# A hybrid S5 / DeltaNet step in which tanh results stay in PSUM, per-head scalings run on ScalarE, inverse blocks are copied into zeroed tiles, and the S5 scan is laid out by place

## The chip, the core and the metric

The kernel runs on one NeuronCore of a Trainium2 chip. The metric is the device time of one execution in microseconds, as the median of several runs. Engines have the profile's names: PE is TensorE (PEld its weight loads), DVE is VectorE, ACT is ScalarE, POOL is GpSimd, SP issues the DMAs.

## The reference

One layer of a bidirectional hybrid backbone works on 2048 latent tokens and 128 context tokens, all in float32. Cut to what matters here:

```python
proj = jnp.dot(h, w_in)                          # u, z_s5, qkv, z_gdn, beta, a
# S5, per direction d: 32 groups of 64 complex states, over the tokens
h[t] = abar * h[t-1] + (b_re + i*b_im) @ u[t]    # complex, h[-1] = h0
y[t] += c_re @ h_re[t] - c_im @ h_im[t]
s5 = gelu(y + u * d_skip) * sigmoid(z_s5)
# gated DeltaNet, per direction: 4 heads of 128, over chunks
q, k, v = split(silu(conv3(qkv)))
m = tril_strict((k * beta) @ k.T * exp(gcum_i - gcum_j))
t_inv = inverse(eye + m)                         # then one state update a chunk
out = concat(s5, gdn) @ w_out; x += gate * out; x += gate * mlp(x)
```

The outputs are both token blocks after a last norm and the context's final states. In the reference the DeltaNet chunks have 64 tokens; the kernel's have 128.

## The kernel before

A first pass makes the normalized tokens, splits them into a high and a low float32r part, stores both in DRAM, and computes u; beside it `s5_setup` and `s5_tables` make the S5 tables and store them (`sp`, `stab`). A second stage computes the other projections in token groups: `group_proj` takes a column tile of the input weights (split the same way, stored in DRAM once and loaded again for later groups), runs 24 matmuls into a PSUM bank of the tile `d` (L471), and `evac` empties it. For q, k and v `evac` applies a three-tap convolution and SiLU: ACT scales the middle tap (L491), DVE adds the two others (L493, L495), ACT takes tanh (L497), DVE combines (L499), and the result goes to DRAM.

Beside the projections run, in steps interleaved by generators with rates (`Side`): the S5 scan (`s5_part`, eight parts of four groups), the first half of DeltaNet (`gdn_first`: transposes, key products, decays; `gdn_p2`: inversion of 32x32 diagonal blocks on DVE; `gdn_p3`: assembling the 128x128 inverses on PE) and later the chunk steps (`gdn_load`, `gdn_step`). The last stage is the output projection and the MLP, with the remaining chunk steps in its beginning. The framework orders each engine's queue by a simulated timeline; an engine then works its queue in order.

`s5_part` covers 2176 tokens as 272 columns of 8 tokens. WI @ u fills S (L1283, evacuated by L1287): eight rows of 272 (direction, re/im, group pair). The rows are cut into 17 blocks of 16 places. Step 1 runs over the places: for `kk` 1 to 15, all 17 blocks at once are multiplied (L1301) and added twice (L1303, L1305), so these instructions take every 16th element. Step 2 carries the state over the blocks, 15 serial steps of three small instructions on `Hin` (L1323 to L1326). Step 3 adds carry times power to every place: POOL multiplies (L1335), DVE adds (L1338), eight times. Then a few state columns are overwritten (L1343, L1344), and L1356 reads the rows out as the moving operand of CA, with L1351 for the direct part; ACT and DVE apply gelu.

In `gdn_back` ACT makes the decays E (L696), POOL multiplies them by beta (L697), DVE multiplies by the key products (L700). In `gdn_p3` POOL writes the diagonal 32x32 blocks RW into the block tiles TA and R by multiplying with block masks Mh and Mb (L762, L764), which also writes the zeros. In `gdn_load` POOL scales the keys of a loaded chunk (L873).

Of the kernel before, what the change touches and what calls it, by code (L numbers as in the profile page):

```python
# [478 lines left out]
def evac(k, ct, ps, n, segs, off):  # L479
# [71 lines left out]
def gdn_setup(k):  # L551

    nc = k.nc
    k.Mb = k.ga.tile([128, 4], F32, name="Mb")
# [14 lines left out]
    nc.gpsimd.memset(k.Mb, 0.0)  # L569
    nc.gpsimd.memset(k.Mh, 0.0)  # L570
    for b in range(4):
        nc.gpsimd.memset(k.Mb[32 * b:32 * b + 32, b:b + 1], 1.0)
        nc.gpsimd.memset(k.Mh[32 * b:32 * b + 32, b % 2:b % 2 + 1], 1.0)
# [108 lines left out]
def gdn_back(k, b, c):  # L682
# [6 lines left out]
    for d in range(2):  # L689
# [7 lines left out]
        nc.gpsimd.tensor_tensor(E, E, bc4(bb[:, d]), op=OP.mult)  # L697
# [51 lines left out]
def gdn_p3(k, cs):  # L749
# [114 lines left out]
def gdn_load(k, c, d, second):  # L864
# [180 lines left out]
def s5_setup(k):  # L1045
# [208 lines left out]
def s5_part(k, hb):  # L1254
# [617 lines left out]
```

## Time and profile before

| | |
|---|---|
| median of 3 runs | 3313.9 us (3308.9 to 3318.6) |
| the profiled execution | 3305.3 us |
| its span | 3303.5 us |
| mean granted clock of PE over the span | 0.95 |

The span is what the profiler recorded from the first instruction to the last; the profiled execution is one run, and its durations are those that the rows below show. An instruction's row gives its line in the kernel, the engine, what it writes and reads, and partitions x elements. "Idle before" is the time in which the engine stood still ahead of such instructions, with the releasers after it.

### The profile page before, as it was taken

The page shows a single profiled execution, that of the slowest core. Times are in us where ns is not written, and L with a number is a line of the kernel's source. Part 1 is how long each engine was busy: PE and PEld are TensorE (multiplying, and loading weights), DVE is VectorE, ACT ScalarE, POOL GpSimd, SP SyncE. Part 2 cuts the span into 40 slices and gives each one's busy share as a digit, 9 for nine tenths or more (in the row PEclk, how much of TensorE's full clock was granted, in tenths as well). Part 3 has the DMA queues.
Part 4 walks back from the last instruction along what each step waited for, and adds up shares of the span by engine and source line. Part 5 has one row for each costly group of instructions (what it writes and reads, how often), then busy time and mean ns, then how long its engine had stood idle before and what let it go on. Part 6 is the DMA issues. An engine that isn't in the chain of part 4 may idle for free.

```text
span 3303.5 us, 53799 instructions
## 1 busy us (share of the span) xinstructions
PE 2998.2 (91%) x19962; PEld 2637.7 (80%) x19962; DVE 2060.2 (62%) x4093; ACT 1115.0 (34%) x2517; POOL 1370.5 (41%) x1027
## 2 busy tenths in 40 slices
PE   5775879999798899988999999999999999999998
PEld 3673668787787777977997899898798898899997
DVE  4965587896876775346555368543368652685555
ACT  3432224443443221245323243322243332432332
POOL 3552232433345242155443453434444444554442
PEclk8887889998997999998999999999999999999999
DMA  9899966867677988999333545222435334453322
GB/s 258 197 179 250 335 205 228 266 217 236 201 217 233 285 286 273 345 307 312 107 103 112 156 147 178 81 76 92 143 99 184 112 102 127 155 166 93 99 90 71
DMA packets 573527, 604.69 MB, mean 183 GB/s; under 512 B 163020, under 2 KB 422208, under 8 KB 573264
## 3 DMA queue, kind: packets, MB, share of 16 engines
q1 hardware_dynamic: 573264, 601.25, 59.4%
q8 instruction: 157, 2.57, 0.3%
q14 instruction: 106, 0.87, 0.1%
HBM read 458.99 MB, written 142.14 MB: 182 GB/s over the span
## 4 chain that ended last, share of the span: by engine, by line
PE 56%; DVE 19%; DMA 14%; issue 4%; ACT 3%; POOL 3%; SPq 2%; POOLq 0%; DVEq 0%; ACTq 0%
PE gA L1523 20%; PE gA L1545 18%; PE d L471 6%; PE gA L1437 3%; PE gs L1356 1%; DVE W L738 1%; DVE Tt L1301 1%; DMA x<-in_posr 1%; DVE UB L736 1%; DMA woraw<-in_w_out 1%; DVE S L1338 1%; PE gs L1283 1%; POOL wol L1400 1%; DVE S L1303 1%; DMA s_stab<-WI 1%
## 5 line engine op out<-in xcount | busy, mean ns | idle before, releaser
L1400 POOL TENSOR_TENSOR wol<-woraw,woh 128x512 fp32r<-128x512 f32 x320 | 426.3, 1343 | 679.9 <-ACT woh L1399 669.5
L1530 DVE TENSOR_TENSOR r<-r 128x256 f32<-128x256 f32 (+1 forms) x256 | 290.7, 1168 | 363.8 <-ACT ffH L1529 363.6
L1399 ACT ACTIVATE woh<-woraw 128x512 fp32r<-128x512 f32 x320 | 194.4, 628 | 794.6 <-PE gA L1545 462.0
L1545 PE MATMUL gA<-woh,ffH 128*128 128x512 f32 x1088 | 426.8, 392 | 8.8 <-ACT r L1527 4.8
L1545 PE MATMUL gA<-woh,ffL 128*128 128x512 f32 x1088 | 425.3, 391 | 1.1 <-DVE ffL L1531 1.1
L1545 PE MATMUL gA<-wol,ffH 128*128 128x512 f32 x1088 | 424.2, 390 | 0.0
L1550 DVE TENSOR_TENSOR acc<-acc,gA 128x512 f32<-128x512 f32 x510 | 336.1, 681 | 123.7 <-PE gA L1545 123.6
L1400 POOL TENSOR_TENSOR wil<-wiraw,wih 128x1024 fp32r<-128x1024 f32 x128 | 318.9, 2491 | 148.5 <-PE gA L1523 111.6
L1523 PE MATMUL gA<-htH,wih 128*128 128x256 f32 (+1 forms) x2048 | 286.9, 292 | 6.0 <-DVE acc L1550 4.0
L1523 PE MATMUL gA<-htL,wih 128*128 128x256 f32 (+1 forms) x2048 | 284.8, 290 | 0.0
L1523 PEld LDWEIGHTS gA<-htH,wih 128*128 128x128 f32 x2048 | 273.0, 192 | 13.1 <-DVE acc L1550 6.3
L1523 PE MATMUL gA<-htH,wil 128*128 128x256 f32 (+1 forms) x2048 | 282.0, 290 | 0.0
L1523 PEld LDWEIGHTS gA<-htL,wih 128*128 128x128 f32 x2048 | 270.5, 192 | 0.9
L1523 PEld LDWEIGHTS gA<-htH,wil 128*128 128x128 f32 x2048 | 268.6, 191 | 0.1
L471 PE MATMUL d<-hH,wh 128*128 128x258 f32 (+3 forms) x1152 | 213.4, 327 | 51.5 <-DMA wh<-s_wc 15.9
L1545 PEld LDWEIGHTS gA<-woh,ffH 128*128 128x128 f32 x1088 | 204.8, 188 | 52.7 <-ACT r L1527 6.1
L471 PEld LDWEIGHTS d<-hH,wh 128*128 128x128 f32 x1152 | 180.2, 206 | 74.0 <-issue 31.4
L1545 PEld LDWEIGHTS gA<-wol,ffH 128*128 128x128 f32 x1088 | 204.7, 188 | 43.2
L1545 PEld LDWEIGHTS gA<-woh,ffL 128*128 128x128 f32 x1088 | 204.9, 188 | 41.4 <-DVE ffL L1531 1.9
L471 PE MATMUL d<-hL,wh 128*128 128x258 f32 (+3 forms) x1152 | 213.1, 320 | 2.7 <-DMA hL<-s_hL 2.7
L471 PE MATMUL d<-hH,wl 128*128 128x258 f32 (+3 forms) x1152 | 209.4, 319 | 4.6 <-DMA wl<-s_wc 4.6
L471 PEld LDWEIGHTS d<-hH,wl 128*128 128x128 f32 x1152 | 178.0, 201 | 18.2 <-issue 10.3
(387 smaller groups left out, 5340.0 us busy)
## 6 DMA issues: line engine op xcount, KB each, us to landing
wiraw<-in_w_mlp_in SPq DMA_DIRECT2D x128, 512.0 KB
woraw<-in_w_mlp_out SPq DMA_DIRECT2D x256, 256.0 KB
wl<-s_wc SPq DMA_DIRECT2D x68, 512.0 KB
wh<-s_wc SPq DMA_DIRECT2D x68, 512.0 KB
wada<-in_w_ada SPq DMA_DIRECT2D x48, 512.0 KB
KVr<-s_kv SPq DMA_DIRECT2D x34, 512.0 KB
Qr<-s_qkv SPq DMA_DIRECT2D x32, 512.0 KB
woraw<-in_w_out SPq DMA_DIRECT2D x64, 256.0 KB
```

Of the source, the lines that this page charges most:

```text
L471: nc.tensor.matmul(ps[:, 0:w], W_[:, kk, :], X_[kk][:, f:f + w], start=(n == 0), stop=(n == 23))
L736: nc.vector.tensor_tensor(tv, W[:, 0:i + 1, i:i + 1].to_broadcast([128, i + 1, m]), U2[:, i, None, i + 1:32].to_broadcast([128, i + 1, m]) ...
L738: nc.vector.tensor_tensor(wv, wv, tv, op=OP.subtract)
L1283: nc.tensor.matmul(ps[64 * par:64 * par + 64, 0:272], WI[:, d, ri, g, 64 * par:64 * par + 64], ub[:, 2 * g + par, :], start=True, stop=Tru ...
L1301: V.tensor_tensor(Tt.rearrange("p j (a s)->p j a s", a=8), sview(S, kk, [[0, 2], [272, 8], [16, 17]]), TB8[:, :, :, None].to_broadcast([12 ...
L1399: nc.scalar.activation(h[:, i:i + n], w, AF.Copy)
L1400: sub.tensor_tensor(l[:, i:i + n], w, h[:, i:i + n].bitcast(F32), op=OP.subtract)
L1437: nc.tensor.matmul(ps, X[:, q, s], W[:, kk, :], start=(q == 0 and m == 0), stop=(q == 7 and m == 2))
L1523: nc.tensor.matmul(ps[b][:, 0:w], W[:, kk, :], X[:, kk, b * w:b * w + w], start=(m == 0), stop=(m == 23))
L1530: nc.vector.tensor_tensor(r[:, 0:w], r[:, 0:w], r[:, 0:w], op=OP.mult)
L1545: nc.tensor.matmul(ps, X[:, s], W[:, hf], start=(m == 0), stop=(m == 3 * FB - 1))
L1550: nc.vector.tensor_tensor(accs[i][:, c], accs[i][:, c], ps, op=OP.add)
```

## The change

1. `evac`: tanh is written to the PSUM bank that the projection came from, and L499's successor reads it there; the SBUF tile is no longer used for it.
2. `gdn_back` and `gdn_load`: the multiplications by beta and by the key decay move from one POOL instruction over four heads to four ACT copies with a per-partition scale.
3. `gdn_p3`: TA and R become tiles that are zeroed once in `gdn_setup`; ACT copies the diagonal blocks to their places, 12 small copies for each pair of chunks. The masks go.
4. `s5_part`: a row is kept by place, 17 places of 17 columns (place 0 holds the state that enters a block, places 1 to 16 follow, the blocks being neighbours), rows are 289 long and ordered re/im, direction, group. The steps over places work on runs of 17 neighbours. The carry over blocks is a doubling scan of 4 steps with the 16th, 32nd, 64th and 128th block powers, on runs of 15, 14, 12 and 8. L1287's successor writes, and L1356's successor reads, the row in token order, that is, one element every 17.
5. `s5_setup`: five tables laid out for direct use instead of two; three complex products for the higher powers. The per-part table copies go.

```diff
@@ -493,10 +493,10 @@
-        th = k.pe.tile([128, k.pew], F32, name="ec2")
-        nc.scalar.activation(th[:, 0:n], y2[:, 0:n], AF.Tanh)
+        th = ps[:, 0:n]
+        nc.scalar.activation(th, y2[:, 0:n], AF.Tanh)
...
-        nc.vector.scalar_tensor_tensor(o_[:, 0:n], th[:, 0:n], 1.0, y2[:, 0:n], op0=OP.add, op1=OP.mult)
+        nc.vector.scalar_tensor_tensor(o_[:, 0:n], th, 1.0, y2[:, 0:n], op0=OP.add, op1=OP.mult)
@@ -551,8 +551,10 @@
+    k.TA = k.ga.tile([128, 2, 4, 64], F32, name="TA")
+    k.R = [k.ga.tile([128, 2, 4, 128], F32, name=f"R{d}") for d in range(2)]
+    for t in (k.TA, *k.R):
+        nc.gpsimd.memset(t, 0.0)
@@ -694,7 +691,8 @@
         for h in range(4):
...
-        nc.gpsimd.tensor_tensor(E, E, bc4(bb[:, d]), op=OP.mult)
+        for h in range(4):
+            nc.scalar.activation(E[:, h], E[:, h], AF.Copy, scale=bb[:, d, h:h + 1])
@@ -753,19 +751,19 @@
-    TA = k.ga.tile([128, 2, 4, 64], F32, name="TA")[:, 0:n]
-    R = [k.ga.tile([128, 2, 4, 128], F32, name=f"R{d}")[:, 0:n] for d in range(2)]
+    TA = k.TA[:, 0:n]
+    R = [r[:, 0:n] for r in k.R]
...
-        for d in range(2):
-            pairs, a, e = PAIRS[d]
-            nc.gpsimd.tensor_tensor(TA[a, j].rearrange("p h (b c)->p h b c", b=2), RW[a, j, d, 1, :, None, :].to_broadcast([64, 4, 2, 32]),
-                                    k.Mh[a, None, :, None].to_broadcast([64, 4, 2, 32]), op=OP.mult)
-            nc.gpsimd.tensor_tensor(R[d][:, j].rearrange("p h (b c)->p h b c", b=4), RW[:, j, d, 0, :, None, :].to_broadcast([128, 4, 4, 32]),
-                                    k.Mb[:, None, :, None].to_broadcast([128, 4, 4, 32]), op=OP.mult)
...
     def sl(blk):
...
+    for d in range(2):
+        pairs, a, e = PAIRS[d]
+        for blk in range(4):
+            nc.scalar.activation(R[d][sl(blk), :, :, sl(blk)], RW[sl(blk), :, d, 0], AF.Copy)
+            if sl(blk).start in (a.start, a.start + 32):
+                nc.scalar.activation(TA[sl(blk), :, :, sl(blk % 2)], RW[sl(blk), :, d, 1], AF.Copy)
...
     for d in range(2):
@@ -870,7 +868,8 @@
-    nc.gpsimd.tensor_tensor(KV[:, 0], KV[:, 0], bc4(k.kd[:, c, d]), op=OP.mult)
+    for h in range(4):
+        nc.scalar.activation(KV[:, 0, h], KV[:, 0, h], AF.Copy, scale=k.kd[:, c, d, h:h + 1])
@@ -1030,13 +1029,13 @@
-    k.tab8 = SP[:, 1088:1216].rearrange("p (j r c)->p j r c", j=2, r=2)
-    k.tabL = SP[:, 1216:1344].rearrange("p (j r c)->p j r c", j=2, r=2)
-    k.h0 = SP[:, 1344:1408].rearrange("p (r c)->p r c", r=2)
...
+    k.tabs = SP[:, 1088:1728].rearrange("p (e b j q)->p e b j q", e=5, b=8, j=2)
+    k.h0 = SP[:, 1728:1792].rearrange("p (r c)->p r c", r=2)
@@ -1124,11 +1123,20 @@
-    for t_, e in ((k.tab8, 1), (k.tabL, 16)):
-        nc.vector.tensor_copy(t_[:, 0, 0], P8[:, 0, :, e])
-        nc.vector.tensor_copy(t_[:, 0, 1], P8[:, 0, :, e])
-        nc.vector.tensor_copy(t_[:, 1, 0], P8[:, 1, :, e])
-        nc.vector.tensor_scalar(t_[:, 1, 1], P8[:, 1, :, e], -1.0, None, op0=OP.mult)
+    Ls = p.tile([128, 2, 4, 32], F32, name="Ls")
+    nc.vector.tensor_copy(Ls[:, :, 0], P8[:, :, :, 16])
+    for i in range(3):
+        cmul(nc.vector, Ls[:, 0, i + 1], Ls[:, 1, i + 1], Ls[:, 0, i], Ls[:, 1, i], Ls[:, 0, i], Ls[:, 1, i], tmp[:, :, 0])
...
+    for e in range(5):
+        re_, im_ = [(P8[:, r, :, 1] if e == 0 else Ls[:, r, e - 1]).rearrange("p (d b g)->p b d g", d=2, b=8) for r in range(2)]
...
+        def to(j, r):
+            return k.tabs[:, e, :, j].rearrange("p b (r d g)->p b r d g", r=2, d=2)[:, :, r]
+        nc.vector.tensor_copy(to(0, 0), re_)
+        nc.vector.tensor_copy(to(0, 1), re_)
+        nc.vector.tensor_copy(to(1, 0), im_)
+        nc.vector.tensor_scalar(to(1, 1), im_, -1.0, None, op0=OP.mult)
@@ -1283,65 +1291,61 @@
-                o = S[:, r + 1:r + 273]
-                nc.scalar.activation(o if d == 0 else o[:, ::-1], ps[:, 0:272], AF.Copy)
+                o = sview(E, r + 17, [[1, 17], [17, 16]]) if d == 0 else sview(E, r + 288, [[-1, 17], [-17, 16]])
+                nc.scalar.activation(o, ps[:, 0:272].rearrange("p (s c)->p s c", c=16), AF.Copy)
...
-        return t.rearrange("p r (d c)->p d r c", d=2)[:, :, :, c0:c0 + 2]
-    TB8 = sb.tile([128, 2, 8], F32, name="tb8", bufs=1)
-    TBL = sb.tile([128, 2, 8], F32, name="tbL", bufs=1)
-    for t_, s_ in ((TB8, k.tab8), (TBL, k.tabL)):
-        for j in range(2):
-            V.tensor_copy(t_[:, j].rearrange("p (d r g)->p d r g", d=2, r=2), cols(s_[:, j]))
+        return t.rearrange("p r (d c)->p r d c", d=2)[:, :, :, c0:c0 + 2]
...
+    def tab(e, n):
+        return k.tabs[:, e, hb, :, :, None].to_broadcast([128, 2, 8, n])
...
-        V.tensor_tensor(Tt.rearrange("p j (a s)->p j a s", a=8), sview(S, kk, [[0, 2], [272, 8], [16, 17]]), TB8[:, :, :, None].to_broadcast([128, 2, 8, 17]), op=OP.mult)
-        av = sview(S, 1 + kk, [[16, 136]])
-        V.tensor_tensor(av, av, Tt[:, 0], op=OP.add)
-        sv = sview(S, 1 + kk, [[1088, 2], [544, 2], [16, 34]])
-        V.tensor_tensor(sv, sv, Tt[:, 1].rearrange("p (d r a)->p d r a", d=2, r=2)[:, :, ::-1], op=OP.add)
+        V.tensor_tensor(Tt.rearrange("p j (a s)->p j a s", a=8), sview(E, 17 * kk, [[0, 2], [289, 8], [1, 17]]), tab(0, 17), op=OP.mult)
+        av = sview(E, 17 * kk + 17, [[289, 8], [1, 17]])
+        V.tensor_tensor(av, av, Tt[:, 0].rearrange("p (a s)->p a s", a=8), op=OP.add)
+        sv = sview(E, 17 * kk + 17, [[1156, 2], [289, 4], [1, 17]])
+        V.tensor_tensor(sv, sv, Tt[:, 1].rearrange("p (r a s)->p r a s", r=2, a=4)[:, ::-1], op=OP.add)
...
+    Hin = sb.tile([128, 144], F32, name="Hin", bufs=1)
+    V.memset(Hin, 0.0)
+    V.tensor_copy(sview(Hin, 1, [[72, 2], [36, 2], [18, 2]]), cols(k.h0))
...
-    Hin = sb.tile([128, 2, 2, 2, 17], F32, name="Hin", bufs=1)
-    H0 = Hin.rearrange("p d r g s->p (d r g s)")
-    V.memset(sview(H0, 16, [[52, 2], [17, 4]]), 0.0)
...
-    def hat(s_):
-        return sview(H0, s_, [[69, 2], [17, 4]])
...
-    def hat3(s_):
-        return sview(H0, s_, [[69, 2], [34, 2], [17, 2]])
-    V.tensor_copy(hat3(0), cols(k.h0))
-    for sc in range(15):
-        Tb = sb.tile([128, 2, 8], F32, name="Tb", bufs=1)
-        V.tensor_tensor(Tb.rearrange("p j (d a)->p j d a", d=2), sview(H0, sc, [[0, 2], [69, 2], [17, 4]]),
-                        TBL.rearrange("p j (d a)->p j d a", d=2), op=OP.mult)
-        V.tensor_tensor(hat(sc + 1), sview(S, 1 + sc * 16 + 15, [[1088 + 16, 2], [272, 4]]), Tb[:, 0].rearrange("p (d a)->p d a", d=2), op=OP.add)
-        V.tensor_tensor(hat3(sc + 1), hat3(sc + 1), Tb[:, 1].rearrange("p (d r g)->p d r g", d=2, r=2)[:, :, ::-1], op=OP.add)
+        V.tensor_copy(sview(Hin, 36 * d + 2, [[72, 2], [18, 2], [1, 15]]), sview(E, row(d, 0, 0) + 272 + d, [[1156, 2], [289, 2], [1, 15]]))
...
+    for i in range(4):
+        sh = 1 << i
+        n = 16 - sh
+        Tb = sb.tile([128, 2, 136], F32, name="Tt", bufs=1)[:, :, 0:8 * n].rearrange("p j (a s)->p j a s", a=8)
+        V.tensor_tensor(Tb, sview(Hin, 1, [[0, 2], [18, 8], [1, n]]), tab(1 + i, n), op=OP.mult)
+        hv = sview(Hin, 1 + sh, [[18, 8], [1, n]])
+        V.tensor_tensor(hv, hv, Tb[:, 0], op=OP.add)
+        hv = sview(Hin, 1 + sh, [[72, 2], [18, 4], [1, n]])
+        V.tensor_tensor(hv, hv, Tb[:, 1].rearrange("p (r a) s->p r a s", r=2)[:, ::-1], op=OP.add)
...
+    def enter(d, ri):
...
+        return (ri * 4 + d * 2) * 18 + 1 - d
...
-                tab = k.P8[:, j, cs, 1:17]
-                T1 = sb.tile([128, 2, 17, 16], F32, name="T1", bufs=2)
-                nc.gpsimd.tensor_tensor(T1, Hin[:, d, ri, :, :, None].to_broadcast([128, 2, 17, 16]),
-                                        tab[:, :, None, :].to_broadcast([128, 2, 17, 16]), op=OP.mult)
-                sv = sview(S, row(d, oi, 0) + 1, [[1, 544]])
-                V.tensor_tensor(sv, sv, T1.rearrange("p g s k->p (g s k)"), op=OP.subtract if ri == 1 and j == 1 else OP.add)
+                t = k.P8[:, j, cs, 1:17]
+                T1 = sb.tile([128, 2, 16, 17], F32, name="T1", bufs=2)
+                nc.gpsimd.tensor_tensor(T1, sview(Hin, enter(d, ri), [[18, 2], [0, 16], [1, 17]]),
+                                        t[:, :, :, None].to_broadcast([128, 2, 16, 17]), op=OP.mult)
+                sv = sview(E, row(d, oi, 0) + 17, [[289, 2], [1, 272]])
+                V.tensor_tensor(sv, sv, T1.rearrange("p g k s->p g (k s)"), op=OP.subtract if ri == 1 and j == 1 else OP.add)
+        V.tensor_copy(sview(E, row(d, 0, 0), [[1156, 2], [289, 2], [1, 17]]), sview(Hin, enter(d, 0), [[72, 2], [18, 2], [1, 17]]))
...
-    for d in range(2):
-        lat, ctx = (0, 256) if d == 0 else (16, 0)
-        V.tensor_copy(sview(S, row(d, 0, 0) + lat, [[544, 2], [272, 2]]), k.h0[:, :, 16 * d + c0:16 * d + c0 + 2])
-        V.memset(sview(S, row(d, 0, 0) + ctx, [[272, 4]]), 0.0)
@@ -1352,8 +1356,8 @@
-                h = S[la, r:r + 272]
-                nc.tensor.matmul(y, CA[la, ri, d, g, :], h if d == 0 else h[:, ::-1],
+                h = sview(E[la], r, [[1, 17], [17, 16]]) if d == 0 else sview(E[la], r + 271, [[-1, 17], [-17, 16]])
+                nc.tensor.matmul(y, CA[la, ri, d, g, :], h,
```

Lines left out: the removal of the masks, the wider SP tile, the loads at the head of `s5_part`.

## Rows read from the trace of the kernel before

**Rows 1.** The page's busy time, share of the span and instructions of each engine
```profile
PE 2998.2 (91%) x19962; PEld 2637.7 (80%) x19962; DVE 2060.2 (62%) x4093; ACT 1115.0 (34%) x2517; POOL 1370.5 (41%) x1027
```

**Rows 2.** Busy time by stretch; behind it granted clock, DMA share, GB/s
```profile
290.00:1300.00 1010.00, 874.56 (x6844) 731.22 (x6845) 750.70 (x1906) 354.91 (x941) 349.46 (x300) 0.91 0.78 249
1300.00:1560.00 260.00, 227.90 (x1431) 209.42 (x1430) 120.31 (x279) 96.53 (x275) 104.00 (x90) 0.94 0.96 327
1560.00:3303.00 1743.00, 1698.57 (x10233) 1532.22 (x10231) 983.93 (x1390) 557.70 (x1102) 774.10 (x484) 0.99 0.39 120
```

**Rows 3.** The chain that ended last, by line, in 290 to 1300 us
```profile
by line: PE d L471 15.8%; issue 5.8%; PE gs L1356 4.6%; DVE W L738 3.6%; DVE Tt L1301 3.6%; DVE UB L736 3.3%; DVE S L1338 3.2%; PE gs L1283 3.1%; DVE S L1303 2.9%; DVE S L1305 2.8%; DMA UB<-s_ub 2.4%; DVE ec L493 2.1%; DVE ec L499 2.0%; DVE
```

**Rows 4.** Waits of PE and its loads, 290 to 1300: total us, times, longest
```profile
PE gs L1356 <- DVE S L1344: 18.9, 9, 4.7
PE d L471 <- DVE ec L495: 15.0, 4, 7.5
PEld d L471 <- ACT ec L491: 24.8, 5, 8.4
```

**Rows 5.** Groups by line and shape, 290 to 1300: busy us, mean ns | idle before
```profile
L1301 DVE TENSOR_TENSOR Tt<-S,tb 128x272 f32<-128x272 f32 x120 | 79.3, 661 | 39.0 <-ACT S L1287 37.0
L1303 DVE TENSOR_TENSOR S<-S,Tt 128x136 f32<-128x136 f32 x120 | 66.4, 554 | 2.3
L1305 DVE TENSOR_TENSOR S<-S,Tt 128x136 f32<-128x136 f32 x120 | 55.3, 461 | 1.9
L1323 DVE TENSOR_TENSOR Tb<-Hin,tbL 128x16 f32<-128x16 f32 x120 | 30.5, 254 | 1.3
L1356 PE MATMUL gs<-S,CA 64*128 64x272 f32 x256 | 59.7, 455 | 18.9 <-DVE S L1344 18.9
```

**Rows 6.** Tile S, whole run: ns min/median/max
```profile
L1301 DVE TENSOR_TENSOR Tt<-S,tb x120: 583/620/1618, 312.9 to 1238.6; 128x272 f32<-128x272 f32 x120
L1303 DVE TENSOR_TENSOR S<-S,Tt x120: 376/401/2470, 314.2 to 1239.3; 128x136 f32<-128x136 f32 x120
L1325 DVE TENSOR_TENSOR Hin<-S,Tb x120: 154/168/2351, 338.4 to 1255.6; 128x8 f32<-128x8 f32 x120
L1338 DVE TENSOR_TENSOR S<-S,T x64: 708/1472/2929, 351.1 to 1271.9; 128x544 f32<-128x544 f32 x64
L1356 PE MATMUL gs<-S,CA x256: 389/389/819, 359.4 to 1289.5; 64*128 64x272 f32 x128
```

**Rows 7.** Tile E, whole run, the same columns
```profile
L697 POOL TENSOR_TENSOR E<-E,bb x34: 1035/1089/1597, 533.4 to 1093.0; 128x512 f32<-128x512 f32 x34
L700 DVE TENSOR_TENSOR Us<-KG,E x34: 672/684/1550, 537.7 to 1097.7; 128x512 f32<-128x512 f32 x34
```

**Rows 8.** More groups by line and shape, 290 to 1300
```profile
L499 DVE SCALAR_TENSOR_TENSOR ec<-ec,ec 128x256 f32<-128x256 f32 x84 | 45.5, 541 | 22.6 <-DMA s_qkv<-ec 13.3 <-ACT ec L497 8.8
L508 DVE SCALAR_TENSOR_TENSOR ec<-ec,d 128x256 f32<-128x256 f32 x8 | 3.4, 421 | 6.2 <-ACT ec L506 6.1
L742 ACT ACTIVATE UB<-W 128x1024 f32<-128x1024 f32 x5 | 10.4, 2078 | 11.0 <-DVE W L738 11.0
L403 ACT ACTIVATE wh<-wraw 128x1024 fp32r<-128x1024 f32 x20 | 21.0, 1053 | 17.1 <-DMA wraw<-in_w_in 7.3 <-PE d L471 6.5 <-DMA s_qkv<-ec 3.3
L764 POOL TENSOR_TENSOR R<-RW,Mb 128x512 f32<-128x512 f32 x34 | 37.0, 1100 | 4.8 <-DVE Tt L1301 3.7 <-DMA s_inv<-R 0.4
```

**Rows 9.** PE in time, 617 to 620: start us, us, what
```profile
618.44 1.19 PE L1356 MATMUL gs<-S,CA 64*128 64x272 f32 x8 [0.55 <-DVE S L1344]
```

**Rows 10.** Scaling on ACT from SBUF to SBUF, line 973: ns min/median/max
```profile
L973 ACT ACTIVATE o<-o,ors x68: 385/388/406, 1376.5 to 1776.8; 128x128 f32<-128x128 f32 x68
```

**Rows 11.** Waits of POOL, 290 to 1560
```profile
POOL KVr L873 <- DMA KVr<-s_kv: 66.4, 18, 7.9
POOL TA L762 <- DMA RW<-s_rw: 27.5, 4, 11.0
```

**Rows 12.** Line 1128 in the setup: ns min/median/max
```profile
L1128 DVE COPY SP<-SP x2: 177/179/181, 111.3 to 132.3; 128x32 f32<-128x32 f32 x2
```

More of the change, by code (lines that the diff above doesn't have):

```diff
@@ L568, in gdn_setup @@
     nc.vector.tensor_copy(k.rsel, sel)
[L569 to L573, printed above, removed]
 def gdn_scalars(k, b):
@@ L981 @@
 PI = float(np.pi)
-SCRATCH_S = {'ys': [512, 8, 272], 'stab': [4, 128, 5120], 'sp': [128, 1408]}
+SCRATCH_S = {'ys': [512, 8, 272], 'stab': [4, 128, 5120], 'sp': [128, 1792]}
 def exp_acc(k, out, x, tag):
@@ L1032, in lane_tables @@
     k.P8 = SP[:, 0:1088].rearrange("p (r c e)->p r c e", r=2, c=32)
-    k.tab8 = SP[:, 1088:1216].rearrange("p (j r c)->p j r c", j=2, r=2)
-    k.tabL = SP[:, 1216:1344].rearrange("p (j r c)->p j r c", j=2, r=2)
-    k.h0 = SP[:, 1344:1408].rearrange("p (r c)->p r c", r=2)
+    k.tabs = SP[:, 1088:1728].rearrange("p (e b j q)->p e b j q", e=5, b=8, j=2)
+    k.h0 = SP[:, 1728:1792].rearrange("p (r c)->p r c", r=2)
 def s5_load(k):
-    SP = k.sp.tile([128, 1408], F32, name="SPl")
+    SP = k.sp.tile([128, 1792], F32, name="SPl")
     k.nc.sync.dma_start(SP, k.S['sp'])
@@ L1065, in s5_setup @@
     lre, lim, ldt = lanes[:, 0], lanes[:, 1], lanes[:, 2]
-    SP = p.tile([128, 1408], F32, name="SP")
+    SP = p.tile([128, 1792], F32, name="SP")
     lane_tables(k, SP)
@@ L1267, in s5_part @@
     nc.sync.dma_start(CA.rearrange("p r d g c->p (r d) (g c)"), dap(k.S['stab'], base + 2048 + hf * 256, [[5120, 128], [512, 4], [1, 256]]))
-    WE = sb.tile([128, 2, 17, 16], F32, name="T1", bufs=2).rearrange("p a b c->p (a b c)")[:, 0:512].rearrange("p (g e c)->p g e c", g=4, e=8)
+    WE = sb.tile([128, 2, 16, 17], F32, name="T1", bufs=2).rearrange("p a b c->p (a b c)")[:, 0:512].rearrange("p (g e c)->p g e c", g=4, e=8)
     nc.sync.dma_start(WE.rearrange("p g e c->p (g e c)"), dap(k.S['stab'], base + 4096 + hf * 512, [[5120, 128], [1, 512]]))
@@ L1271, in s5_part @@
     nc.scalar.activation(WT, WE.rearrange("p g e c->p g c e"), AF.Copy)
-    S = su.tile([128, 1 + 8 * 272], F32, name="S")
+    E = su.tile([128, 8 * 289], F32, name="S")
     def row(d, ri, g):
-        return (d * 4 + ri * 2 + g) * 272
+        return (ri * 4 + d * 2 + g) * 289
     for g in range(2):
@@ L1308, in s5_part @@
     for d in range(2):
-        V.tensor_copy(k.NS[:, :, 16 * d + c0:16 * d + c0 + 2], sview(S, row(d, 0, 0) + 272 - 256 * d, [[544, 2], [272, 2]]))
-    Hin = sb.tile([128, 2, 2, 2, 17], F32, name="Hin", bufs=1)
-    H0 = Hin.rearrange("p d r g s->p (d r g s)")
-    V.memset(sview(H0, 16, [[52, 2], [17, 4]]), 0.0)
-    def hat(s_):
-        return sview(H0, s_, [[69, 2], [17, 4]])
-    def hat3(s_):
-        return sview(H0, s_, [[69, 2], [34, 2], [17, 2]])
-    V.tensor_copy(hat3(0), cols(k.h0))
@@ new lines, in s5_part @@
+        V.tensor_copy(k.NS[:, :, 16 * d + c0:16 * d + c0 + 2], sview(E, row(d, 0, 0) + 272 + 16 - 16 * d, [[1156, 2], [289, 2]]))
+    for i in range(4):
[7 more added lines that the diff above has]
+        V.tensor_tensor(hv, hv, Tb[:, 1].rearrange("p (r a) s->p r a s", r=2)[:, ::-1], op=OP.add)
```

2 lines of the change are left out of this document (removed).

## Prediction

> **What bounds the kernel now.** I read the busy times first. TensorE is busy 91% of the span, VectorE 62% [rows 1]. That is a mean over unlike stages, so the table by stretch comes next [rows 2]. From 1560 us on, TensorE is busy 1699 of 1743 us at a granted clock of 0.99: nothing that the change touches there can move much. In 1300 to 1560 the DMA engines are busy 0.96 of the time. From 290 to 1300, where nearly all edits lie, no engine is full: TensorE 875 of 1010 us, VectorE 751, ScalarE 355, GpSimd 349, and the clock is only 0.91. TensorE idles 135 us there.
>
> The chain of that stretch [rows 3] shows what sets its pace. TensorE's projection (L471) has 15.8%; the scan's VectorE lines have 3.6, 2.9 and 2.8% (the three of each step) and 3.2% (the carry-in add), the scan's read-out L1356 has 4.6%. So chained VectorE work and TensorE take turns. The waits say the same: TensorE waits 18.9 us for the last write of a scan, 15.0 us for L495 and 24.8 us (its loads) for L491 to give a bank back [rows 4]. What VectorE gives up is thus worth something, but not one for one: the three step lines have 9.3% of 1010 us, 94 us, on the chain and 201 us busy [rows 5]. That ratio, 0.47, is what I count of a saved VectorE microsecond. L1356 has 46 us on the chain of 60 us busy [rows 3, 5]: 0.78 for TensorE's.
>
> **Scan steps.** Before, a step touches every 16th element (64 bytes apart); after, runs of 17 neighbours. A two-operand instruction on 8 elements takes 154 ns [rows 6], one on 512 unbroken elements 672 [rows 7]: 1.03 ns an element on 146 ns. By this the 272-element multiply should take 426 and each 136-element add 286 ns; they take 583 and 376 at best [rows 6], (583 - 146)/272 = 1.61 ns an element. So I put the extra down to the stride. At the fastest times of the rows, 583 and twice 376 against 426 and twice 286 saves 337 ns a step, 120 steps: 40 us. At the means (661, 554, 461 [rows 5]), shrunk in the same ratio, 0.25 x 1676 x 120: 50 us. I take 45.
>
> **Carry chain.** 15 serial steps of three tiny instructions become 4 doubling steps. Before: 15 x 3 x 154 ns = 6.9 us a part at best, 15 x 3 x 254 = 11.4 us at the mean [rows 5, 6]. After: 12 instructions x 146 ns, plus 1.03 ns for 32 x (15 + 14 + 12 + 8) elements: 3.4 us at best, 5.6 in the same ratio. Over eight parts 28 to 46 us; I take 37. Beside it, table copies, memsets and end-state copies leave and four small copies a part come: about 1 us less each, 6 to 8 us in all; 6.
>
> **tanh in PSUM.** L499 reads two SBUF operands and takes 541 ns; L508, the same shape with one in PSUM, 421 [rows 8]: 84 x 0.12 = 10 us of VectorE. The bank is now held until L499 has read it, two instructions later than now. Three banks cover that while a group of 24 matmuls and what lies between is longer than the added hold; I charge 1 us, and 15 if the 15.0 us wait [rows 4] doubles.
>
> VectorE together: 45 + 37 + 6 + 10 = 98 us, times 0.47: **-46 us**. The ends are 0 (all of it covered) and 98.
>
> **The price on TensorE.** The read-out's moving operand was contiguous and becomes one element every 68 bytes. No matmul in this trace reads so. Eight passes of 272 columns now run in 1.19 us, one alone 389 ns [rows 6, 9]: (1.19 - 0.39)/7 = 0.114 us a pass, 29 us for 256. No row excludes that nothing is lost. From above: if each column takes the 1.61 ns that VectorE needs for a far element, a pass takes 0.438 us and 256 of them 83 us more. By ratio the rows ask less: VectorE 1.61 against 1.03, and ScalarE's transposing copy of 1024 elements 2078 ns against 1053 for a straight one [rows 8], about 2. I take twice, the nearer in kind since every engine in these rows slowed by about that: 29 us more, x 0.78: **+23 us** (0 to +65).
>
> [...]
>
> The same operand is written by ScalarE at 68 bytes (L1287, 64 times). Doubled per element, as L742 is, that is 64 x 0.25 = 16 us of an engine busy 35% of the stretch; I charge 1.
>
> **GpSimd to ScalarE.** The GpSimd work that leaves is E x beta (34 x 1.09 us, 37 us), the R blocks (37 us) [rows 7, 8], the smaller TA products and, later, the key decay. GpSimd and VectorE slow each other: the carry-in add L1338, issued beside GpSimd's product, has a median of 1472 ns against 708 at best [rows 6]. With some 75 us less GpSimd in this stretch from E and R alone I take **-10 us** (0 to -25).
>
> ScalarE takes four copies of 128x128 for each E and each KV, 388 ns a copy [rows 10]: 136 x 0.39 = 53 us apiece, and 12 small copies for each pair of chunks in place of the R and TA products. Four E copies take 1.56 us against 1.09 on GpSimd: 34 x 0.5 = 16 us of latency, hidden now because VectorE has other work in front of L700; I charge 0, and 16 if that cover is gone. The R copies stand on ScalarE ahead of the G copy that L786 waits for: nine calls, at most 12 x 0.39 = 4.7 us each, 42 us; the emitted order can put G first, so 2.
>
> **Waits that move.** GpSimd waits 66.4 us for KV to land and 27.5 us for RW [rows 11], and little hangs on it there. Now ScalarE waits, and queued behind are w (L923), for which L926 on TensorE waits, and the evacuations that free TensorE's banks. Ends: 0 and 94 us; ScalarE is 37% busy in 1300 to 1560 [rows 2], so I take 5.
>
> **Setup.** Three complex products (18 instructions) and 20 copies for 8: 30 more VectorE instructions at about 0.18 us [rows 12], 5 us before the scan tables can be made; 3. The one-time zeroing of three tiles on GpSimd replaces smaller memsets: 0.
>
> **Sum.** -46 + 23 - 10 + 1 (bank) + 1 (L1287) + 2 + 5 + 3 = **-21 us**. The profiled execution took 3305.3 us, its span is 3303.5; it lies 8.6 us under the median of the runs, 3313.9. So the forecast is 3284 for an execution like the profiled one, **3293 us** as the median. A measurement here tells about 0.3%, 10 us, from no change.
>
> **Rivals.**
> *A. The strided operand costs nothing.* [...] For it: half of these operands are read backwards already, and all passes take 389 ns at the least and at the median [rows 6]. Then 3293 - 23 = 3270.
> *B. Slower: a column costs as long as a far element does on VectorE.* Place: L1356, eight bursts of 32 passes in the read-out, at the head of TensorE's queue. For it: 1.61 ns on VectorE and at most 2.03 on ScalarE (2078 ns over 1024 elements) are not far apart; that looks like a time for each access and not a ratio. Against: 0.78 of it must reach the end. 3293 - 23 + 65 = 3335. It decides, that is, takes the gain away, from (21 + 23)/(0.78 x 256) = 0.22 us over the 0.114 us of a pass: 0.33 us a pass, 1.2 ns a column. [...]
> *C. ScalarE blocked by the moved DMA waits.* Half of the 94 us reaching the end instead of 5: 3293 + 42 = 3335. For it: the longest of those waits are 7.9 and 11.0 us [rows 11]. Against: ScalarE idles more than half of both stretches.
> *D. Covered.* VectorE's relief is taken by TensorE and DMA, busy 0.87 and 0.78 of the stretch [rows 2]; half of the 46 us goes: 3316, no change.
>
> **How the numbers follow.** Chances: forecast 0.38, A 0.20, B 0.22, C 0.10, D 0.10. The forecast's own range is 3270 to 3310. The case of the 98 us counted whole (3241) and B and C with their spread set the range: 3240 to 3348. Faster by over 0.3% (under 3304): forecast 0.31, A 0.19, D 0.02, B and C 0.01: 0.53. Within 0.3%: 0.06 + 0.01 + 0.06 + 0.03 = 0.16. Slower: 0.31.
>
> **What would show it.** Right: the three step lines near 430, 290 and 290 ns at their fastest; 32 carry multiplies in place of 120; L1356's passes about 0.23 us apart, at an end near 0.45 us if B holds; VectorE's busy time in the stretch some 100 us less, and TensorE's idle time less by some 40. Wrong: L1356's share of the chain at 10% or more (B); ScalarE waiting tens of us for s_kv and s_rw with w or the bank evacuations behind it (C); VectorE's busy time down and TensorE's idle time not (D).

## The result: slower by 1.6%

The changed kernel takes **3364.0 us** (median of 4 runs, 3353.6 to 3367.5) against 3311.4 us beside it: 1.0159 of the time before, 95% interval 1.0128 to 1.0190, some 52 us more where I had forecast 21 less. Its profiled execution took 3364.5 us, its span is 3362.7.

The page's busy times of the kernel after, to hold against [rows 1]:

```profile
PE 3052.2 (91%) x19962; PEld 2656.4 (79%) x19962; DVE 1971.6 (59%) x3828; ACT 1248.9 (37%) x2897; POOL 1237.7 (37%) x884
```

VectorE is relieved by 89 us and GpSimd by 133, as the change means it. ScalarE has 134 more, and TensorE, which does the same products, 54 more. By stretch, as [rows 2] (busy time of PE, its loads, DVE, ACT, POOL; granted clock, DMA share, GB/s):

```profile
290.00:1300.00 1010.00, 880.06 (x6602) 708.89 (x6603) 642.43 (x1595) 451.35 (x1212) 239.95 (x215) 0.87 0.74 235
1300.00:1560.00 260.00, 231.37 (x1395) 208.45 (x1394) 87.77 (x194) 93.55 (x274) 57.49 (x48) 0.97 0.94 314
1560.00:3362.00 1802.00, 1743.73 (x10511) 1572.99 (x10509) 1026.66 (x1490) 595.91 (x1211) 798.34 (x505) 0.99 0.41 125
```

From 290 to 1300 us TensorE is a little busier than before and gets through 242 instructions fewer (6602 against 6844), at a granted clock of 0.87 against 0.91. VectorE has 108 us less to do there. In the chain of that stretch, as [rows 3], the scan's VectorE lines have less (the step's multiply 2.0% instead of 3.6), and TensorE's have more: the projection 24.7% instead of 15.8, the read-out (L1360) 7.3 instead of 4.6:

```profile
by line: PE d L471 24.7%; PE gs L1360 7.3%; issue 3.8%; PE gs L1291 3.5%; DVE S L1346 2.9%; DMA UB<-s_ub 2.6%; DMA wraw<-in_w_in 2.1%; PE gT L673 2.1%; DVE Tt L1307 2.0%; DMA s_ub<-Us 2.0%; DVE W L736 2.0%; DVE UB L734 1.9%; DMA wh<-s_wc 1.
```

The groups that answer [rows 5, 8] (busy us, mean ns | idle before):

```profile
L1307 DVE TENSOR_TENSOR Tt<-S,SPl 128x272 f32<-128x272 f32 x120 | 62.7, 523 | 21.1 <-ACT S L1295 18.8
L1309 DVE TENSOR_TENSOR S<-S,Tt 128x136 f32<-128x136 f32 x120 | 36.7, 305 | 2.1
L1311 DVE TENSOR_TENSOR S<-S,Tt 128x136 f32<-128x136 f32 x120 | 40.5, 337 | 2.1
L1360 PE MATMUL gs<-S,CA 64*128 64x272 f32 x256 | 100.7, 654 | 15.2 <-DVE S L1346 15.2
L499 DVE SCALAR_TENSOR_TENSOR ec<-d,ec 128x256 f32<-128x256 f32 x84 | 34.9, 415 | 32.9 <-ACT d L497 20.9 <-DMA s_qkv<-ec 11.8
L695 ACT ACTIVATE E<-E,bb 128x128 f32<-128x128 f32 x136 | 46.3, 412 | 0.1
```

And the view of the tile S, as [rows 6] (ns min/median/max):

```profile
L1360 PE MATMUL gs<-S,CA x256: 631/636/819, 344.4 to 1182.0; 64*128 64x272 f32 x128
L1307 DVE TENSOR_TENSOR Tt<-S,SPl x120: 422/441/2611, 312.7 to 1133.1; 128x272 f32<-128x272 f32 x120
L1295 ACT ACTIVATE S<-gs x64: 607/648/698, 304.7 to 1107.7; 128x272 f32<-128x272 f32 x64
L1346 DVE TENSOR_TENSOR S<-S,T x64: 708/1046/2911, 338.8 to 1166.8; 128x544 f32<-128x544 f32 x64
```

The VectorE prices are those forecast: 422 ns for the multiply (426 put), 415 ns for L499 (421). The pass of the read-out is not at 389 ns any more but at 631 and more. The read-out in time, as [rows 9] (start, us, what):

```profile
584.22 2.10 PE L1360 MATMUL gs<-S,CA 64*128 64x272 f32 x8 [0.36 <-DVE S L1346]
609.51 4.03 PE L1360 MATMUL gs<-S,CA 64*128 64x272 f32 x8
```

Eight passes take 2.10 us in one burst, where [rows 9] had 1.19, and 4.03 in another. The waits, to hold against [rows 4, 11], of PE in 290 to 1300 us and of ACT in 290 to 1560 (total us, times, longest):

```profile
PE d L471 <- DVE ec L499: 23.3, 7, 8.1
PEld d L471 <- DVE ec L499: 21.1, 6, 9.0
PE gs L1360 <- DVE S L1346: 15.2, 7, 6.5
PE g L773 <- DMA RW<-s_rw: 8.7, 2, 7.6
ACT KVr L872 <- DMA KVr<-s_kv: 40.1, 13, 8.9
ACT R L764 <- DMA RW<-s_rw: 13.7, 3, 11.6
```

The new waits that the prediction priced are there: the bank held until L499, and ScalarE waiting for s_kv and RW. Whether they cost the 52 us, or the read-out does, or something that no row names, is what the experiments had to tell.

### The profile page after: what moved, and what is told of

It is laid out like the page before. It is cut to its first block, busy times and chain, and to the rows that moved or that the text cites. A ratio compares the mean times of both kernels' runs of the same rounds, so it can differ in the third digit from the quotient of the medians.

```text
span 3362.7 us, 53572 instructions
## 1 busy us (share of the span) xinstructions
PE 3052.2 (91%) x19962; PEld 2656.4 (79%) x19962; DVE 1971.6 (59%) x3828; ACT 1248.9 (37%) x2897; POOL 1237.7 (37%) x884
## 4 chain that ended last, share of the span: by engine, by line
PE 62%; DMA 14%; DVE 13%; ACT 3%; issue 3%; SPq 2%; POOL 2%; POOLq 0%; DVEq 0%; ACTq 0%
PE gA L1527 19%; PE gA L1549 18%; PE d L471 10%; PE gA L1441 3%; PE gs L1360 2%; PE gs L1291 1%; DVE otmp L1461 1%; DMA KVr<-s_kv 1%; DMA wh<-s_wc 1%; DVE S L1346 1%; DMA s_stab<-WI 1%; DMA wraw<-in_w_in 1%; DMA x<-in_x_sample 1%; DMA UB<-s_ub 1%; DMA x<-in_posr 1%
## 5 line engine op out<-in xcount | busy, mean ns | idle before, releaser
L471 PE MATMUL d<-hH,wh 128*128 128x258 f32 (+3 forms) x1152 | 221.5, 334 | 45.8 <-DVE ec L499 23.3
L471 PEld LDWEIGHTS d<-hL,wh 128*128 128x128 f32 x1152 | 176.1, 199 | 23.8 <-issue 11.8
```

The lines of the kernel that those rows point to most:

```text
L471: nc.tensor.matmul(ps[:, 0:w], W_[:, kk, :], X_[kk][:, f:f + w], start=(n == 0), stop=(n == 23))
```

## The experiments

Four theories: **read-out** (the strided operand costs more than I put), **bank** (tanh in PSUM holds the projection's bank), **ScalarE** (the moved copies and their waits), **run-ahead** (a shorter scan lets its TensorE work stand ahead of the projections in the queue). Each ratio is to the kernel before, run beside it, with its 95% interval. Where two variants were run at different times, I compare their ratios, and give the difference in us of 3303.

**One part alone.** The change has parts that stand on their own: before plus the scan (`scan_only`), plus tanh in PSUM (`tanh_only`), plus the ScalarE copies (`act_only`). And the changed kernel with an unstrided read-out (`contig`):

```diff
-                h = sview(E[la], r, [[1, 17], [17, 16]]) if d == 0 else sview(E[la], r + 271, [[-1, 17], [-17, 16]])
+                h = E[la, r:r + 272] if d == 0 else E[la, r:r + 272][:, ::-1]
```

> The kernel before with the scan's part of the change alone (layout by place, doubling carry chain, strided write and strided read-out), tanh and GpSimd's products as before. Theory ScalarE (the moved copies and their DMA waits cost the 52 us): the scan alone keeps my prediction's terms, -46 + 23, so 3275 to 3300. Theory bank (tanh in PSUM holds the projection's bank and costs the 52 us): the same, 3275 to 3300. Theory read-out (the strided operand, 41 us more busy TensorE, is what costs): 3330 to 3360. Theory run-ahead (a shorter scan only lets its TensorE work crowd in ahead of the projections): 3310 to 3350, with the scan's last part ending some 100 us earlier and the last projection not earlier.

> The kernel before with tanh written back to its PSUM bank, and nothing else changed. Theory bank: the projection waits 20 to 45 us for the final VectorE read of the bank in place of the read two instructions earlier, and the time is 3330 to 3360. Theories ScalarE, read-out and run-ahead: -5 to +3 us, 3306 to 3315.

> The kernel before with the work moved from GpSimd to ScalarE alone: E scaled by four copies, R and TA copied by blocks into zeroed tiles, KV scaled by four copies. Theory ScalarE: 3335 to 3365, with the waits for s_kv and RW on ScalarE's queue and ScalarE's evacuation of the projections later. Theories bank, read-out and run-ahead: 3300 to 3316 (GpSimd's relief against some waits).

> The changed kernel, but the scan's read-out takes 272 neighbouring elements as its moving operand, so that its columns come in the order of the scan's layout and not of the tokens (this part of the computation is changed); all other work is the same. Theory read-out: a pass falls from 0.21 to 0.11 us, and the time by 30 us or more, to 3325 to 3335. Theories bank, ScalarE and run-ahead: at most 15 us less, 3350 to 3365.

Measured: scan alone 3361.5 us, 1.0179 (1.0148 to 1.0210); tanh 3322.3, 1.0056 (1.0033 to 1.0078); ScalarE 3315.7, 1.0043 (1.0022 to 1.0064); contiguous 3316.7, 1.0041 (1.0023 to 1.0058). Bank and ScalarE fall as the main cause: the scan alone has the whole loss. Each is still slower by itself, by some 19 and 14 us; tanh lies between what its own theory and what the others allowed. The unstrided read-out gives 39 us of it back (1.0159 less 1.0041, of 3303), more than theory read-out asked.

**The price by itself, a reordered load, and the rate.** `before_strided` is the kernel before with the changed kernel's access in L1356 and nothing else. `place` (before plus the scan) and `place_all` (the whole change) put u in place order once a part, so that neither ScalarE nor TensorE has a stride. `late` changes one number, the scan's rate in the interleaving of the generators:

```diff
-                h = S[la, r:r + 272]
+                h = sview(S[la], r, [[1, 17], [17, 16]]) if d == 0 else sview(S[la], r + 271, [[-1, 17], [-17, 16]])
...
+    for q in range(4):
+        nc.gpsimd.tensor_copy(ub[:, q].rearrange("p (c s) -> p c s", c=16), ut[:, q].rearrange("p (s c) -> p c s", c=16))
...
-            scans = Side(2, [s5_part(k, hb) for hb in range(8)])
+            scans = Side(1.7, [s5_part(k, hb) for hb in range(8)])
```

> The kernel before, but the scan's read-out takes its 272 columns with the changed kernel's access (16 runs of elements 17 apart, on the old layout, so its columns come in a wrong order: this part of the computation is changed); all other work is the same. Theory price (the strided operand alone costs TensorE what the changed kernel lost, and VectorE's relief is worth about nothing): +40 to +50 us, 3343 to 3353 on a before of 3303. Theory sum (the operand costs about 100 us and VectorE's relief gives back 46): 3390 to 3410. Theory small price (my +23 holds and the loss is in the order of the work): 3320 to 3330.

> The kernel before with the scan's new layout and carry chain, but u is put in place order once per part by four GpSimd copies; so the scan's rows are written and read out without a stride, and the last gelu step writes its result back in token order. tanh and GpSimd's products as before. Theory price: the whole relief of VectorE and no price, yet 3295 to 3310, since the relief is worth about nothing. Theory sum: 3250 to 3270. Theory small price with run-ahead (the shorter scan crowds in ahead of the projections): 3310 to 3340.

> The changed kernel with the same reordering of u and no stride at TensorE or ScalarE; tanh in PSUM and ScalarE's copies stay. Theory price: 3310 to 3320, as the variant with contiguous read-out (3317). Theory sum: as that variant too. If the strided write by ScalarE costs as well: 3290 to 3305.

> The changed kernel with the scan's rate in the interleaving lowered from 2 to 1.7 steps for each projection step, so that its read-outs stand further back in TensorE's queue; nothing else is changed, the strided read-out stays. Theory run-ahead: the projections lose less, 3325 to 3345. Theory price: the same strided passes run anyway, 3350 to 3365.

Measured: the access alone makes the old kernel 3355.3 us, 1.0168 (1.0149 to 1.0186), 52 us more. Its queues hold the same instructions in the same order as before's, so this is a price and no reordering. But `late`, with all its strided passes, takes 3299.1 us, 0.9993 (0.9982 to 1.0003): one number gives the whole loss back. `place` is 3328.7, 1.0087 (1.0069 to 1.0104), `place_all` 3306.0, 1.0024 (1.0004 to 1.0044). So neither theory price nor theory run-ahead has it alone.

**Is the rate a repair?** Control: the kernel before at 1.7. With it the unstrided read-out, and both place-order kernels, at 1.7.

> Control: the kernel before with the scan's rate at 1.7 in place of 2, nothing else. If the lower rate repairs what the shorter scan had disturbed (theory run-ahead), the old kernel has nothing to repair and stays within 10 us: 3293 to 3313. If the lower rate is a gain of its own whatever the scan costs: 3245 to 3280.

> The changed kernel at rate 1.7 (3299 us) with the read-out taken from 272 neighbouring elements, so its columns come in a wrong order (this part of the computation is changed); the order of all instructions is the same as in the kernel at 1.7 with the strided read-out. Theory price (45 to 53 us, as in the two pairs so far): 3245 to 3256. If the price hangs on what stands around the read-out and was large only where the projections waited: 3270 to 3290.

> The kernel before with the scan in place order from the load on (no stride at TensorE or ScalarE), at rate 1.7. Theory run-ahead: VectorE's relief comes through once the order is repaired, 3250 to 3275 against 3329 at rate 2. If the relief is worth nothing in any order: 3295 to 3310.

> The whole change with the scan in place order from the load on, at rate 1.7. Theory run-ahead with the price gone: 3240 to 3260. If neither the relief nor the price shows in this order: 3290 to 3306.

Measured: `before_late` 3360.2 us, 1.0177 (1.0156 to 1.0199); `contig_late` 3256.3, 0.9854 (0.9838 to 0.9869); `place_late` 3293.7, 0.9979 (0.9965 to 0.9993); `place_all_late` 3279.5, 0.9927 (0.9911 to 0.9943). The same number that gives the changed kernel 55 us back costs the old one 57. So 1.7 is not a better rate in itself. Is it run-ahead? Counted in the trace, 1743 of the 3456 projection matmuls stand ahead of the end of the fourth part's read-out before the change, 1338 after it, 1693 at 1.7. The place-order kernels go the same way, `place` from 1301 to 1721 and `place_all` from 1361 to 1732. All four kernels with the shorter scan gain by it: 55 us the changed one, 62 the contiguous one (which has its order), 36 and 32 these two. That is what run-ahead says, though both place-order kernels stay behind its forecasts: `place_late`, with the relief and no stride on TensorE or ScalarE, is only 7 us faster than before. But the old kernel at 1.7 has 1751, nearly the old place, and the loss is there. So this count alone does not set the time, and run-ahead is not the whole account; for the shorter scan it is not excluded, and the old kernel was run at no rate above 2. What holds is that one number, by which the framework lays out the queues anew, made four kernels 32 to 62 us faster and the fifth 57 us slower. The price holds in this order too: `contig_late` against `late`, same order of instructions, 46 us.

**What VectorE's relief is worth.** The changed kernel, at either rate, with 14 of 15 scan steps 64 bytes apart as before; the order of all instructions stays as in its partner. `strides` reads the old rows 1, 2, 3, 4, 8, 12, 16 and 17 elements apart, a distance a part. `place_all_15` is `place_all` at 1.5.

```diff
-    for kk in range(1, 16):
+    for kk, o_, p_, w_ in [(kk, 16 + kk, 1, 16) for kk in range(1, 15)] + [(15, 255, 17, 1)]:
...
-        av = sview(E, 17 * kk + 17, [[289, 8], [1, 17]])
+        av = sview(E, o_ + p_, [[289, 8], [w_, 17]])
```

> The changed kernel, but 14 of a part's 15 scan steps take elements 64 bytes apart as the old layout did (the recurrence then runs along other places: this part of the computation is changed). The order of all instructions and their counts are the changed kernel's, so this prices the faster step alone. By my prediction 337 to 420 ns x 112 = 38 to 47 us of VectorE, times 0.47: 18 to 22 us slower, 3372 to 3380. Theory covered (in the changed kernel's order VectorE's relief is worth nothing): at most 8 us slower, 3353 to 3363.

> The changed kernel at scan rate 1.7 with the same slow scan steps, all instructions in the order of the kernel at 1.7 (3299 us). By my prediction's share of 0.47: 3317 to 3323. If the relief is worth more where TensorE's idle time is small (theory run-ahead: at 1.7 the relief comes through): 3325 to 3345. Covered: 3297 to 3305.

> The kernel before, with the read-out of the eight parts taking elements 1, 2, 3, 4, 8, 12, 16 and 17 apart (its data are then mixed up: this part of the computation is changed), one look for the time of a pass of 272 columns at each distance. [...] Theory any stride: 0.21 from 2 on. Theory far element: growing up to 8 or 16 elements.

> The whole change with the scan in place order from the load on, at scan rate 1.5 instead of 1.7 (3279 us) or 2 (3306 us). If the best place of the read-outs in TensorE's queue is the one they had before the change, 3260 to 3280; if the order's effect has no such optimum, anywhere from 3270 to 3330.

Measured: `after_slow` 3377.7 us, 1.0218 (1.0192 to 1.0244); `late_slow` 3322.1, 1.0046 (1.0031 to 1.0062). Against their partners (1.0159 and 0.9993) that is 0.59 and 0.53%, 19 and 18 us, with the intervals taken together some 13 and 6 us either way. The groups of `after_slow` give the VectorE time for it:

```profile
L1307 DVE TENSOR_TENSOR Tt<-S,SPl 128x272 f32<-128x272 f32 x120 | 78.5, 654 | 21.2 <-ACT S L1295 18.9
L1309 DVE TENSOR_TENSOR S<-S,Tt 128x136 f32<-128x136 f32 x120 | 52.5, 438 | 2.1
L1311 DVE TENSOR_TENSOR S<-S,Tt 128x136 f32<-128x136 f32 x120 | 52.1, 434 | 2.1
```

183.1 us in place of 139.9 in the changed kernel: 43 us of VectorE for 19 us of time, a share of 0.45 (at 1.7: 0.41). That agrees with my 0.47, as far as such intervals can tell, and "covered" falls. `place_all_15` took 3286.7, 0.9940 (0.9916 to 0.9963): no better than at 1.7.

The bursts of eight passes of `strides`, one of 2, 4, 8 and 16 elements apart, all four at a granted clock of 1.00 (the profiled execution took 3338.3 us):

```profile
461.30 1.32 PE L1356 MATMUL gs<-S,CA 64*128 64x272 f32 x8 [0.26 <-DVE S L1344]
...
761.85 2.18 PE L1356 MATMUL gs<-S,CA 64*128 64x272 f32 x8 [2.63 <-DVE S L1344]
...
926.57 2.21 PE L1356 MATMUL gs<-S,CA 64*128 64x272 f32 x8
...
1199.47 2.09 PE L1356 MATMUL gs<-S,CA 64*128 64x272 f32 x8
```

At 3 elements the fastest burst took 1.75 us, at neighbours 1.19 [rows 9]. So a burst costs about a tenth more at 2 elements (1.32 us), 1.8 times as much at 4 (2.18), and about the same at 8 and 16 (2.21 and 2.09). That is neither theory any stride, which had the whole price from 2 on, nor theory far element, which had it growing up to 8 or 16. Why the price comes between 2 and 4 elements no run shows.

**A version without the stride.** In the order of `late`: the read-out contiguous, so its columns come in place order; the direct product (L1355) reads u with a stride, 64 passes in place of 256; the last gelu step writes back in token order. And the same with tanh in SBUF.

```diff
-        nc.tensor.matmul(y, WT[:, g4].rearrange("p c e->p (c e)"), ub[:, g4, :], start=True, stop=False)
+        nc.tensor.matmul(y, WT[:, g4].rearrange("p c e->p (c e)"), ub[:, g4].rearrange("p (s c)->p c s", c=16), start=True, stop=False)
...
-        V.scalar_tensor_tensor(Y[:, g4], a, 1.0, y, op0=OP.add, op1=OP.mult)
+        V.scalar_tensor_tensor(Y[:, g4].rearrange("p (s c)->p c s", c=16), a.rearrange("p (c s)->p c s", c=16), 1.0, y.rearrange("p (c s)->p c s", c=16), op0=OP.add, op1=OP.mult)
```

> A version meant to be better: the changed kernel at scan rate 1.7 with the read-out contiguous; its columns come in place order, the direct product WT takes u with a stride (64 passes strided in place of 256), and the last gelu step writes its result back in token order. By the pair at 1.7 (3299 strided, 3256 contiguous) with a quarter of the strided passes back, about 11 us, and some 0.15 us more in 32 VectorE writes: 3262 to 3276. If the strided write on VectorE delays the part's store: up to 3290.

> The same with tanh in SBUF as in the kernel before, so that the projection's bank comes free two instructions earlier. The framework lays out another order. If the bank's wait (23 us on TensorE in the changed kernel) is worth what it lasts: 3240 to 3262. If the order decides: anywhere from 3260 to 3320.

Measured: 3275.5 us, 0.9911 (0.9886 to 0.9935), and 3284.8, 0.9941 (0.9918 to 0.9963). The first is the fastest of the kernels that compute the whole reference, with `place_all_late` (0.9927) within its interval; both beat the kernel before. tanh in SBUF was not faster, in an order of its own, so the bank's wait shows no cost here that stands out from the order.

## Why the prediction was wrong

Two things failed: the term for the strided operand was half of what it is, and there was no term for the order of the queues.

**The price on TensorE (+23) is the step that failed.** I put a pass at twice, 29 us for 256 passes, and 0.78 of it on the end. Three pairs with one order of instructions give the time: 52 us in the old kernel, 39 in the changed one, 46 at 1.7 (46 in the mean; their intervals are 6 to 12 us either way). The busy time that I put and the share of it that reaches the end were both low. The windows of the projection stage, from its first to its last matmul, in the old kernel and with the stride alone:

```profile
327.00:1414.00 1087.00, 964.03 (x7499) 829.67 (x7499) 774.82 (x1972) 375.05 (x1019) 365.27 (x309) 0.92 0.79 255
```

```profile
325.00:1472.00 1147.00, 1034.78 (x7499) 860.84 (x7498) 772.76 (x1970) 374.81 (x1019) 363.96 (x309) 0.89 0.74 241
```

The read-out's group in the second:

```profile
L1356 PE MATMUL gs<-S,CA 64*128 64x272 f32 x256 | 100.3, 656 | 18.8 <-DVE S L1344 18.8
```

The read-out itself is 41 us busier (59.7 to 100.3), not 29. I had taken 0.114 us a pass from one burst [rows 9] for all 256; [rows 5], with 59.7 us for them, spoke against it, twice my 29. There are two kinds of burst. In one the passes start in pairs, 13 ns apart, and eight of neighbours take 1.19 us; in the other, 16 of the 32 bursts, they start singly, 0.229 us apart, and eight take 2.10. Why some come in pairs no run shows. The clock is not the difference, as its column shows (after the burst's window: its time, its passes' busy time, that of their loads, the granted clock, DMA). In the old kernel, pairs and singles at the upper level of the clock, and pairs at the lower:

```profile
618.44:619.63 1.19, 1.19 (x8) 0.70 (x8) 1.00 0.56 178
640.79:642.89 2.10, 2.10 (x8) 1.42 (x8) 1.00 0.69 205
1057.68:1059.87 2.19, 2.19 (x8) 1.21 (x8) 0.50 0.83 292
```

With the stride alone, the same three, and singles at the lower level; then singles of neighbours at the lower level, from `contig`:

```profile
647.83:649.93 2.10, 2.10 (x8) 0.74 (x8) 1.00 1.07 408
654.97:658.90 3.93, 3.93 (x8) 1.51 (x8) 1.00 0.78 254
1093.51:1095.71 2.20, 2.20 (x8) 1.16 (x8) 0.50 0.75 240
659.81:663.83 4.02, 4.02 (x8) 2.35 (x8) 0.50 0.91 315
```

```profile
799.93:803.92 3.99, 3.99 (x8) 2.50 (x8) 0.50 0.98 307
```

So the stride nearly doubles both kinds at a granted clock of 1.00, from 1.19 to 2.10 us and from 2.10 to 3.93, and costs next to nothing at 0.50 (2.19 and 2.20, 3.99 and 4.02): a far operand takes at either level about what neighbours take at the lower one. A single pass then takes 0.46 us. The ratio of the rows (about two) was right, and so was rival B's rate of 0.44 us for such a pass, its sign beside the forecast's; its 83 us were too many, since a burst of pairs loses half as much and one at the lower level next to nothing; L1360's share of the chain stayed at 7.3%, under the 10% that it named. Its break-even of 0.33 us a pass stood on the same 0.114.

And TensorE is 71 us busier, not 41: the granted clock is 0.89 instead of 0.92, and the other matmuls take 30 us more. In the records of the clock, all 16 single bursts of the old kernel ran at 1.00; with the stride 4 of 16 did, in 7 the clock fell during the burst, and 5 ran at 0.50 from their start. TensorE's idle time in the stage, 123 us, shrinks only to 112. So 41 us of the read-out came to the end as 52, not as 0.78 of it.

**The missing term.** The same windows of the changed kernel at rates 2 and 1.7, and of the old one at 1.7:

```profile
327.00:1471.00 1144.00, 1020.03 (x7499) 848.77 (x7499) 674.09 (x1676) 489.22 (x1344) 249.41 (x188) 0.89 0.76 243
```

```profile
328.00:1421.00 1093.00, 1010.34 (x7499) 843.61 (x7499) 668.80 (x1679) 486.47 (x1342) 246.94 (x188) 0.90 0.79 254
```

```profile
327.00:1474.00 1147.00, 986.07 (x7499) 847.78 (x7499) 761.98 (x1971) 376.55 (x1019) 371.40 (x310) 0.90 0.74 242
```

All three have 7499 matmuls, as before. TensorE's idle time (length less busy) is 124, 83 and 161 us, against 123 before. Of the old kernel's 60 us at 1.7, 38 are idle time and 22 slower matmuls at a lower clock; of the changed kernel's 51, 41 are idle time. Before the change the order was one with little idle time for its work; nothing in the profile before says what another edit's order will be. My sum with the right price would be -21 - 23 + 46 = +2, and the change measured +52 in its own order and -2 at 1.7. Without any price it would be -44, and the contiguous read-out measured +14 and, at 1.7, -48. That both sums are met at 1.7 is luck: nothing in them chose that rate. The some 50 us that miss at rate 2 are of the size of the order's effect; that they are the order is not shown, since an edit of this change can't be made without a new order. Nor is it settled which placement in the queue does it: `late` loses 10 us of waiting for the scan's adds (L1346, 15.2 to 5.5) and 8 for stored weights (10.5 to 2.9); `before_late` gains 16 of the latter (15.9 to 32.1). The rest are many small waits.

**VectorE (-46): right in its busy time, and in its share where that was measured.** The steps fell from 201 to 140 us, more than the 45 put; the carry chain from 90 to 33, not by 37 but by 57; L499 by the 10. These three make 129 us; the whole stretch has 108 us less VectorE, I said 98. The share was measured at 0.41 and 0.45 for the steps alone; that the carry chain's 57 us reach the end in the same share was not tested.

**The small terms.** L1295 takes 648 ns where its line took 398 (64 x 0.25 = 16 us of ScalarE, the bound). L1346's median fell from 1472 to 1046 ns with GpSimd relieved, as argued; its price alone was not measured. The cover of the E copies was thinner than I said: L698 waited 17.9 us for them (before, L700's 3.5 us of idle time had other causes), about the 16 us I named for that case. ScalarE waits 57 us for KV and RW, of 94 at most (rival C), and TensorE 8.7 for RW; `act_only` lost 14 us with all of that, in an order of its own, so C is bounded and not priced. The bank, +1 in the sum, has TensorE waiting 23.3 us for L499 where 15.0 were for L495, and `tanh_only` lost some 19, again in an order of its own: more than I charged, perhaps, and not priced either. Rival D's sign is there, TensorE's idle time in 290 to 1300 us is 130 us against 135, but `after_slow` and `late_slow` show that the relief is worth its time; D falls. Rival A falls by the pass times at the upper level of the clock (2.10 us a burst against 1.19).

## What to carry to other kernels

A layout that helps one engine can cost the others that write and read it (here 41 us more of read-out on TensorE, and 648 ns in place of 398 for ScalarE's write): put the reordering where it touches the fewest elements (here 64 passes of the direct product instead of 256 of the read-out). On the engine that sets the pace, price a slower operand at full weight and with the other work that slows down with it (here 41 us of read-out and 30 of other matmuls, for 52 us of time), and take the time of an instruction from all its bursts, against the busy time of its group, not from one. Where a framework lays out the queues anew, an edit's time holds its order's effect: compare in pairs whose instructions stand in one order, and try a few rates on both sides before calling a change good or bad.

## What the runs showed of the hardware

The read-out's moving fp32 operand took TensorE 1.32 us for eight paired passes of 272 columns at 2 elements' distance, about a tenth more than the 1.19 for neighbours, and 2.1 to 2.2 at 4, 8, 16 and 17, all at a granted clock of 1.00; at 3 the fastest burst took 1.75. At a clock of 0.50 the stride of 17 made next to no difference (2.20 us against 2.19). VectorE's multiply of 272 elements took 583 ns at its fastest at 16 elements' distance and 422 for neighbours; by element that is 1.61 ns against 1.03, my estimate from [rows 6, 7], a factor of 1.6. ScalarE's write at 17 took 648 ns for 272 elements against 398, 1.6 too, while TensorE's factor was 1.8 on a burst. And the granted clock moved with it: 0.92 to 0.89 in the projection stage, for the strided operand alone, with the other matmuls 30 us busier.
